# A two-layer hybrid decoder step on one core: full-height second score product, prompt values in one stage, norms first among the background stages

## The chip, the cores and the metric

The kernel runs on one core of one Trainium2 chip. The metric is the time of one execution in device microseconds (us). PE is TensorE (matmuls), DVE is VectorE, ACT is ScalarE, POOL is GpSimd and SP is SyncE, which here only issues transfers. PSUM is the memory that PE writes its results to; DVE and ACT read them from there.

## The reference, cut to what matters

One step of a two-layer decoder trunk for a prompt of 512 tokens and 32 sample tokens: layer 0 mixes tokens by gated linear attention, layer 1 by dilated windowed attention with three groups of heads, and each is followed by a gated convolutional feed-forward block. The change is in layer 1. Its scores, for each head and each group:

```python
DIL_GROUPS = ((128, 1), (512, 4), (2048, 16))          # (window, dilation)
q, k = _rmsnorm(p[:, :, :, 0], q_gain), _rmsnorm(p[:, :, :, 1], k_gain)   # per head, 64 wide
s = jnp.einsum('bhqe,bhke->bhqk', qb, kw) * DIL_SCALE + bias
p = jnp.exp(s - jnp.max(s)); den = jnp.sum(p)
o = jnp.einsum('bhqk,bhke->bqhe', p, vw) / den
out = sum over groups of softmax(log den + max) * o       # then @ w_out
```

(This is the reference's `_dil_group_prompt` and `_combine_groups` with the reshaping taken out.)

## The kernel before, in words

All activations stand transposed, 128 features on the partitions and 544 tokens (512 prompt, 32 sample) in the columns. Weights and activations are split into two float32r halves, high and low, and `product` (line 104) multiplies three of the four combinations: per block of 128 output columns of a weight and per half of the tokens it issues 24 matmuls into one PSUM buffer, tagged `ps` (three buffers). After every three of its eight steps of the contraction it calls `tick()`.

`tick()` runs the background work. There are four queues of generators, `lanes[0]` to `lanes[3]`; a tick takes them from the last to the first and lets the head of each go on to its next `yield`. Before the change `lanes[3]` holds `values`, `lanes[2]` the norms, `lanes[1]` the decode work on the key and value caches, `lanes[0]` the `attention` of one head pair and one group. The order in which instructions stand on an engine follows from the ticks and from the scheduler of the tile layer, which moves ready instructions past waiting ones; on the chip each engine takes its instructions in that order.

In `dilated` the loop over `jj` (8 head pairs of 2 heads of 64) projects q, k and v of the three groups by `product`, 9 products for each pair. For each pair there are:

- `qk_norm`, six times: the mean square over 64 features by two matmuls with a block matrix (`pn`, lines 694 and 695), a logarithm and an exponential on ACT, a multiplication on DVE.
- `attention`, three times: transposes of v (`pvt`), scores into `psc`, softmax on DVE and ACT into `ex`. For group 0 the scores are made of split operands. `split_scores` builds for each head h a q2 that holds q's high half in this head's 64 rows and q's low half in the other 64, and a k2 that holds k's high half in both, so that one matmul over 128 rows (line 798) gives high times high plus low times high. What is missing, high times low, is a second product over the 64 rows of the head (line 801), with k's low half `kl`. Both heads share one tile `kl`, each in its own 64 rows. The loop over `UNITS[0]` gives 8 matmuls of line 798 and 8 of line 801 for each pair, 2 of the 8 with 128 columns and 6 with 256.
- `values`: the three groups' softmax sums are combined (`share`), `ex` is scaled on DVE (line 873 or so), transposed by PE (`ptr`, line 892), copied from PSUM into `PT` by ACT and DVE (lines 894, 896), and multiplied with the values into one PSUM buffer `po` (line 907), 30 matmuls with 64 output rows. Group 2 uses the tile `diag`, zero outside its small blocks, in place of `PT`. The four units are (group 1), (group 2), (group 0, first half), (group 0, second half), and the line 907 matmuls of the first two stand in stage 3 of the loop over n, those of the other two in stage 5:

```python
for m in {3: (0, 1), 5: (2, 3)}.get(n, ()):
    ...
    mm(o, R[g][2][:, kb, r], PT[m][:, h, c:c + P], start=..., stop=..., skip_group_check=True)
```

So three shapes of the PE array are in use beside the full 128 rows x 128 columns of `product`: 64 rows x 128 columns (lines 796 and 801), 128 rows x 64 columns (line 907), and 128 x 32 or 64 x 32 (decode, lines 949, 959, 1004, 1009; group 2's scores, line 781). A profile row gives the shape as rows*columns.

Of the kernel before, what the change touches and what calls it, by code (L numbers as in the profile page):

```python
# [11 lines left out]
F32 = mybir.dt.float32  # L12
# [7 lines left out]
P = 128  # L20
# [16 lines left out]
def trunk(ctx: ExitStack, tc: tile.TileContext, A, O, stage=4):  # L37
# [23 lines left out]


    lanes = [deque(), deque(), deque(), deque()]
    norms = lanes[2]

    def tick():

# [570 lines left out]
    def dilated(nx, xold, tables, nxt):  # L638
        first = load_w(A["wdi"][0], KT, 256, "wdi")
        with ExitStack() as es:  # L640
# [24 lines left out]
            dma2(dmask, A["dmask"])  # L665
            diag = ac.tile([P, 2, 512], F32, name="diag")
            nc.gpsimd.memset(diag, 0.0)
            done = set()

            def upto(what):  # L670
# [54 lines left out]
            def split_scores(q, k):  # L725


                kl = at.tile([P, TP], F32R, name="kl", bufs=1)
                parts = []
                for h in range(2):  # L730
                    a, b = slice(64 * h, 64 * h + 64), slice(64 - 64 * h, 128 - 64 * h)
                    q2, k2 = [at.tile([P, TP], F32R, name=f"{n}{h}", bufs=1) for n in ("q2", "k2")]
                    nc.scalar.copy(q2[a], q[a])
                    nc.scalar.copy(k2[a], k[a])
                    nc.scalar.copy(k2[b], k[a])
                    tt(out=q2[b], in0=q[a], in1=q2[a].bitcast(F32), op=ALU.subtract)
                    tt(out=kl[a], in0=k[a], in1=k2[a].bitcast(F32), op=ALU.subtract)
                    parts.append((q2, k2, kl))
                return parts

            def softmax(st, h, todo):
# [10 lines left out]
            def attention(jj, g, q, k, v, R):  # L752

                sk, W, R_ = tables[g]
                nk = (256, P, 32)[g]
                bias = at.tile([P, 2, nk], F32, name=f"bias{g}", bufs=1)
                t = sk[:]
                dma(bias, bass.AP(t.tensor, t.offset + 2 * jj * R_ + min(nk, P) - 1, [[W, P], [R_, 2], [1, nk]]))
                vt = at.tile([P, 4, P], F32, name="vt", bufs=4)
                ps = pa.tile([P, 512], F32, name="pvt", tag="pa")  # L760
                for t in range(4):
                    nc.tensor.transpose(ps[:, t * P:(t + 1) * P], v[:, t * P:(t + 1) * P], ident)
                nc.scalar.copy(vt.rearrange("p a b -> p (a b)"), ps)
                yield
                while (jj, 1, g) not in done:
                    yield
                parts = split_scores(q, k) if g == 0 else None
                if parts:
                    yield
                    yield  # L770
                st = at.tile([P, 4, 2, 2], F32, name=f"st{g}")
                ex = []
                if g == 2:
                    ps = [pa.tile([P, 512], F32, name="psc", tag="pa") for h in range(2)]
                    ex.append(at.tile([P, 2, 4, 32], F32, name="ex2", bufs=1))
                    for t in range(4):
                        for h in range(2):
                            r = slice(64 * h, 64 * h + 64)
                            for c in range(4):
                                cc = slice(c * P + 32 * t, c * P + 32 * t + 32)  # L780
                                mm(ps[h][32 * c:32 * c + 32, 32 * t:32 * t + 32], q[r, cc], k[r, cc], start=True, stop=True)
                    for h in range(2):
                        softmax(st, h, [(t, ps[h][:, 32 * t:32 * t + 32], ex[0][:, h, t], bias[:, h]) for t in range(4)])
                        yield
                for u, todo in enumerate(UNITS[g]):
                    ps = [pa.tile([P, 512], F32, name="psc", tag="pa") for h in range(2)]
                    ex.append([at.tile([P, 512], F32, name="ex", bufs=6) for h in range(2)])

                    for part in range(2 if parts else 1):
                        for i, (t, k0, c, w) in enumerate(todo):  # L790
                            tq, tk = slice(t * P, (t + 1) * P), slice(k0 * P, k0 * P + w)
                            for h in range(2):
                                r = slice(64 * h, 64 * h + 64)
                                o = ps[h][:, c:c + w]
                                if not parts:
                                    mm(o, q[r, tq], k[r, tk], start=True, stop=True)
                                elif part == 0:
                                    mm(o, parts[h][0][:, tq], parts[h][1][:, tk], start=(i == 0), stop=False,
                                       skip_group_check=True)
                                else:  # L800
                                    mm(o, parts[h][0][r, tq], parts[h][2][r, tk], start=False, stop=True,
                                       skip_group_check=True)
                    for h in range(2):
                        softmax(st, h, [(t, ps[h][:, c:c + w], ex[u][h][:, c:c + w], bias[:, h, nk - w:])
                                        for t, k0, c, w in todo])
                        yield
                R[g] = (st, ex, vt)
                done.add(("scores", jj, g))
# [19 lines left out]
            def values(jj, R):  # L828
# [31 lines left out]
                for n in range(len(units) + 2):  # L860
# [17 lines left out]
                    if 0 <= n - 1 < len(units):  # L878
                        g, u = units[n - 1]
                        if g < 2:  # L880
                            lo = UNITS[g][u][0][2]
                            PT[n - 1] = at.tile([P, 2, 512], F32, name="PT")
                        else:
                            PT[n - 1] = diag
                            for c in range(4):
                                r = slice(32 * c, 32 * c + 32)
                                nc.vector.transpose(diag[r].rearrange("p h (t c k) -> p (h t) c k", c=4, k=32)[:, :, c],
                                                    R[g][1][0][r].rearrange("p h t k -> p (h t) k"))
                        for h in range(2 if g < 2 else 0):
                            pt = pa.tile([P, 512], F32, name="ptr", tag="pa")  # L890
                            for a in range(lo, 512, P):
                                nc.tensor.transpose(pt[:, a:a + P], R[g][1][u][h][:, a:a + P], ident)
                            if h:
                                nc.scalar.copy(PT[n - 1][:, h, lo:], pt[:, lo:])
                            else:
                                nc.vector.tensor_copy(PT[n - 1][:, h, lo:], pt[:, lo:])
                    for m in {3: (0, 1), 5: (2, 3)}.get(n, ()):
                        g, u = units[m]
                        if po is None:
                            po = pa.tile([P, 512], F32, name="po", tag="pa")  # L900
                        todo = ([(t, k0 + kk, c + kk * P) for t, k0, c, w in UNITS[g][u] for kk in range(w // P)]
                                if g < 2 else [(t, t, t * P) for t in range(4)])
                        for i, (t, kb, c) in enumerate(todo):
                            for h in range(2):
                                r = slice(64 * h, 64 * h + 64)
                                o = po[r, t * P:(t + 1) * P] if g == 0 else po[r].rearrange("p (m c r) -> p r c m", c=4, r=4)[:, t]
                                mm(o, R[g][2][:, kb, r], PT[m][:, h, c:c + P], start=(m == 0 and i == 0),
                                   stop=(m + 1 == len(units)), skip_group_check=True)
# [5 lines left out]
            def decode_scores(j, ks, pace, D):  # L914
# [1 line left out]

                bl = at.tile([P, 3, P], F32, name="bl", bufs=1)
                dma2(bl, A["dbl"][j])
                bh, bx = at.tile([P, 2, 2, P], F32R, name="b2", tag="kl", bufs=1).rearrange("p c g n -> c p g n")
                nc.scalar.copy(bh, bl[:, 1:])  # L920
                tt(out=bx, in0=bl[:, 1:], in1=bh.bitcast(F32), op=ALU.subtract)
                Sd = D["Sd"] = at.tile([P, KEYS], F32, name="Sd", bufs=1)
# [107 lines left out]
            for jj in range(KT):  # L1030
# [8 lines left out]
                for n, (c, g) in enumerate(ORDER):  # L1039
# [46 lines left out]
                    if (c, g) == (2, 2):  # L1086
                        if jj:
                            upto(("values", jj - 1))
                        lanes[3].append(values(jj, R))
                if i:  # L1090
                    lanes[1].append(decode_values(j, vs, 9 if j < 3 else 2, D))
                    upto((jj, 1, 0))
# [4 lines left out]
            ogh = [xp.tile([P, NT], F32R, name=f"xh{k}") for k in range(6)]  # L1097
            ogl = [xp.tile([P, NT], F32R, name=f"xl{k}") for k in range(6)]
            ogh += [at.tile([P, NT], F32R, name="ogh", tag="p", bufs=3) for k in range(2)]
            ogl += [at.tile([P, NT], F32R, name="ogl", tag="PT") for k in range(2)]  # L1100

            def split_og(k):
                nc.scalar.copy(ogh[k], og[k])
# [1 line left out]

            for k in range(6):
                split_og(k)
            spare = [("q20", 1), ("q21", 1), ("k20", 1), ("k21", 1), ("kl", 1)] + 3 * [("q", 3)]
            x = [None] * KT

            def old(m):
# [222 lines left out]
```

## Time and profile before

| what | value |
|---|---|
| median of 3 runs | 1783.75 us (1783.56 to 1787.02) |
| time of the profiled execution | 1782.73 us |
| its span, first to last instruction | 1781.0 us |
| granted TensorE clock, share of full speed | 0.998 |
| PE busy | 1762.5 us, 99% of the span |
| DVE busy | 1088.0 us, 61% |
| ACT busy | 802.6 us, 45% |

The span is cut by the program's stages: the first layer's mixer to about 247 us, its feed-forward block to about 672 us, the dilated layer to about 1385 us, and the last feed-forward block to the end. A matmul's row has its start and its duration from entering the array to its modelled end; matmuls overlap in the array, so the cost of one in a stream is the distance between two starts and not the duration. Plain float32 matmuls leave two records each, transposes and float32r matmuls one.

### The profile page before, as it was taken

Reading aid. Unit: us, or ns where it says so; the run is one execution under the profiler, and the core shown is the slowest. Engines: PE = TensorE matmul, PEld = TensorE weight load, DVE = VectorE, ACT = ScalarE, POOL = GpSimd, SP = SyncE. Lnnn points to the kernel's source line nnn. Section 1 sums busy time; section 2 is a strip of 40 time slices with the busy share of each in tenths; the row PEclk is TensorE's granted clock in tenths of the full one; section 3 lists DMA queues with packets and bytes.
Section 4 is the critical chain, followed back from the end, with each engine's and each line's share of the span. In section 5 each row is a group of like instructions: output and inputs, shape, how many; then the busy total and the mean of one; then the engine's idle time right before and its main releaser. Section 6 shows DMA issues by size and latency. Waiting matters only on the chain. (4 is left out here: it accounts for less than half of the span.)

```text
span 1781.0 us, 35680 instructions
## 1 busy us (share of the span) xinstructions
PE 1762.5 (99%) x14774; PEld 1672.8 (94%) x14774; DVE 1088.0 (61%) x2552; ACT 802.6 (45%) x1549; POOL 225.4 (13%) x416
## 2 busy tenths in 40 slices
PE   7999999999999999999999999999999999999999
PEld 7999999999999999988998889889888999999999
DVE  7665656764467645666575657666665666347652
ACT  5554544442244435645556465537454434224331
POOL 3000101110011110111012010211121111002100
PEclk9999999999999999999999999999999999999999
DMA  5034432432422244346436643654473222222222
GB/s 183 27 136 152 139 120 74 154 105 82 138 92 95 82 139 180 105 168 220 172 118 208 226 150 129 218 180 151 168 253 139 95 77 75 92 101 96 79 97 87
DMA packets 55266, 236.24 MB, mean 133 GB/s; under 512 B 11470, under 2 KB 20896, under 8 KB 37056
## 3 DMA queue, kind: packets, MB, share of 16 engines
q1 hardware_dynamic: 36816, 145.61, 23.6%
q0 software_dynamic: 18288, 88.36, 13.9%
q8 instruction: 116, 1.90, 0.4%
q14 instruction: 46, 0.38, 0.1%
HBM read 210.32 MB, written 29.33 MB: 135 GB/s over the span
## 5 line engine op out<-in xcount | busy, mean ns | idle before, releaser
L104 PE MATMUL ps<-xh,whi 128*128 128x256 f32 (+2 forms) x3056 | 890.1, 292 | 7.4 <-ACT xh L157 5.4
L104 PE MATMUL ps<-xl,whi 128*128 128x256 f32 (+2 forms) x3056 | 885.8, 290 | 4.0 <-DVE xl L158 4.0
L104 PE MATMUL ps<-xh,wlo 128*128 128x256 f32 (+2 forms) x3056 | 885.4, 290 | 0.7 <-DVE wlo L91 0.7
L104 PEld LDWEIGHTS ps<-xh,whi 128*128 128x128 f32 (+1 forms) x3056 | 576.6, 189 | 25.4 <-issue 15.9
L104 PEld LDWEIGHTS ps<-xl,whi 128*128 128x128 f32 (+1 forms) x3056 | 576.4, 189 | 11.7 <-DVE xl L158 5.6
L104 PEld LDWEIGHTS ps<-xh,wlo 128*128 128x128 f32 (+1 forms) x3056 | 576.2, 189 | 8.9 <-issue 5.9
L104 PE MATMUL ps<-gl,whi 128*128 128x272 f32 x704 | 198.8, 287 | 0.0
L104 PE MATMUL ps<-gh,whi 128*128 128x272 f32 x704 | 198.5, 288 | 0.3 <-DVE x L196 0.3
L104 PE MATMUL ps<-gh,wlo 128*128 128x272 f32 x704 | 195.8, 287 | 0.0
L566 DVE TENSOR_TENSOR u<-ps,rstd 128x256 f32<-128x256 f32 x176 | 74.2, 422 | 141.5 <-PE ps L104 141.1
L90 ACT CAST whi<-wu 128x1024 fp32r<-128x1024 f32 x88 | 92.4, 1050 | 98.1 <-PE ps L104 98.1
L104 PEld LDWEIGHTS ps<-gh,whi 128*128 128x128 f32 x704 | 132.2, 188 | 0.5 <-DVE x L196 0.5
L104 PEld LDWEIGHTS ps<-gl,whi 128*128 128x128 f32 x704 | 132.5, 188 | 0.0
L196 DVE TENSOR_TENSOR x<-ps,x 128x272 f32<-128x272 f32 x108 | 46.7, 439 | 140.5 <-PE ps L104 138.9
L104 PEld LDWEIGHTS ps<-gh,wlo 128*128 128x128 f32 x704 | 130.9, 188 | 0.0
L91 DVE TENSOR_TENSOR wlo<-wu,whi 128x1024 fp32r<-128x1024 f32 x88 | 107.5, 1221 | 32.7 <-ACT whi L90 32.6
L90 ACT CAST whi<-wd 128x768 fp32r<-128x768 f32 x64 | 50.1, 783 | 171.5 <-PE ps L104 142.1
L572 POOL COPY uo<-u 128x18 f32<-128x18 f32 x88 | 53.4, 607 | 401.6 <-DVE u L568 401.6
L91 DVE TENSOR_TENSOR wlo<-wdi,whi 128x1024 fp32r<-128x1024 f32 x72 | 87.9, 1221 | 18.3 <-ACT whi L90 18.2
L90 ACT CAST whi<-wdi 128x1024 fp32r<-128x1024 f32 x72 | 75.2, 1045 | 45.6 <-PE ps L104 36.8
L588 ACT CAST gh<-g 128x544 fp32r<-128x544 f32 x44 | 28.5, 647 | 132.5 <-DVE g L585 132.5
L124 ACT ACTIVATE ex<-ex,nm 128x128 f32<-128x128 f32 (+2 forms) x192 | 74.6, 390 | 25.7 <-DVE nm L748 25.7
(307 smaller groups left out, 2371.9 us busy)
## 6 DMA issues: line engine op xcount, KB each, us to landing
wu<-in_wu SPq DMA_DIRECT2D x44, 1024.0 KB, 4.8
wdi<-in_wdi SPq DMA_DIRECT2D x36, 1024.0 KB, 5.2
vc<-in_dv POOLq DMA_DIRECT2D x28, 1024.0 KB, 7.0
wd<-in_wd SPq DMA_DIRECT2D x32, 704.0 KB, 4.1
kc<-in_dkA POOLq DMA_DIRECT2D x16, 1024.0 KB, 6.5
kc<-in_dkB POOLq DMA_DIRECT2D x16, 768.0 KB, 5.2
out_vo<-v POOLq DMA_DIRECT2D x24, 256.0 KB, 3.0
out_ko<-k POOLq DMA_DIRECT2D x24, 256.0 KB, 2.7
```

The costliest lines, as they stand in the source:

```text
L90: nc.scalar.copy(hi, r)
L91: tt(out=lo, in0=r, in1=hi.bitcast(F32), op=ALU.subtract)
L104: mm(ps[:m, :b - a], ww, xx[k][:, a:b], start=(k == 0 and s == 0), stop=(k == kt - 1 and s == 2))
L124: last_exp[0] = act(out, in_, AF.Exp, **kw)
L196: tt(out=out[:, c], in0=ps, in1=old[:, c], op=ALU.add)
L566: tt(out=u[:, 2 + c0:258 + c0], in0=ps[:, :256], in1=nx.rstd[:, c0:c0 + 256], op=ALU.mult)
L572: nc.gpsimd.tensor_copy(out=uo[:, f, :].rearrange("p (b t) -> p b t", t=2), in_=u[:, 512:566].rearrange("p (b t) -> p b t", t=6)[:, :, :2])
L588: nc.scalar.copy(h_, g)
```

## The change

1. The second product of group 0's scores goes over all 128 rows. `kl` becomes two tiles `klz0` and `klz1`, one for each head, that are set to zero once at the start of `dilated` by two ACT copies from the zeroed `diag`; `split_scores` then writes only the head's own 64 rows. Line 801 (802 after) uses q2 and klz whole: the other head's 64 rows of q2 meet zeros.
2. The value products of all four units stand in stage 5. `PT` has three buffers in place of two.
3. The norms go to `lanes[3]` and `values` to `lanes[2]`, so a tick runs the norms first.
4. `b2`, which shared a buffer with `kl`, has its own. SBUF for it comes from the descriptor memory of POOL's transfers, set to 8192 bytes per partition.

```diff
     lanes = [deque(), deque(), deque(), deque()]
-    norms = lanes[2]
+    norms = lanes[3]
...
             nc.gpsimd.memset(diag, 0.0)
+            klz = [ac.tile([P, TP], F32R, name=f"klz{h}") for h in range(2)]
+            for t in klz:
+                nc.scalar.copy(t, diag[:, 0])
...
-                kl = at.tile([P, TP], F32R, name="kl", bufs=1)
...
-                    tt(out=kl[a], in0=k[a], in1=k2[a].bitcast(F32), op=ALU.subtract)
-                    parts.append((q2, k2, kl))
+                    tt(out=klz[h][a], in0=k[a], in1=k2[a].bitcast(F32), op=ALU.subtract)
+                    parts.append((q2, k2, klz[h]))
...
-                                    mm(o, parts[h][0][r, tq], parts[h][2][r, tk], start=False, stop=True,
+                                    mm(o, parts[h][0][:, tq], parts[h][2][:, tk], start=False, stop=True,
                                        skip_group_check=True)
...
-                            PT[n - 1] = at.tile([P, 2, 512], F32, name="PT")
+                            PT[n - 1] = at.tile([P, 2, 512], F32, name="PT", bufs=3)
...
-                    for m in {3: (0, 1), 5: (2, 3)}.get(n, ()):
+                    for m in {5: (0, 1, 2, 3)}.get(n, ()):
...
-                bh, bx = at.tile([P, 2, 2, P], F32R, name="b2", tag="kl", bufs=1).rearrange("p c g n -> c p g n")
+                bh, bx = at.tile([P, 2, 2, P], F32R, name="b2", bufs=1).rearrange("p c g n -> c p g n")
...
-                        lanes[3].append(values(jj, R))
+                        lanes[2].append(values(jj, R))
...
-    nc = bacc.Bacc("TRN2", target_bir_lowering=False, num_devices=1)
+    nc = bacc.Bacc("TRN2", target_bir_lowering=False, num_devices=1, dynamic_dma_scratch_size=8192)
```

The change moves instructions. On PE, in the third head pair (jj = 2) where the first half of group 0's scores stands among the products of a projection, the program has before:

```order
L104 MATMUL ps<-xl_7240,whi 128x272
L798 MATMUL psc<-k_10565,q_10564 128x128
L798 MATMUL psc<-k_10565,q_10564 128x256
L801 MATMUL psc<-kl,q_10564 128x128
L801 MATMUL psc<-kl,q_10564 128x256
L104 MATMUL ps<-xh_7239,wlo 128x272
L104 MATMUL ps<-xh_7327,whi 128x272
L104 MATMUL ps<-xl_7328,whi 128x272
L104 MATMUL ps<-xh_7327,wlo 128x272
L104 MATMUL ps<-xh_7415,whi 128x272
L798 MATMUL psc<-k_10572,q_10571 128x128
```

and now (line numbers one higher):

```order
L104 MATMUL ps<-xh_7239,wlo 128x272
L799 MATMUL psc<-k_10566,q_10565 128x128
L799 MATMUL psc<-k_10566,q_10565 128x256
L802 MATMUL psc<-klz_7650,q_10565 128x128
L802 MATMUL psc<-klz_7650,q_10565 128x256
L104 MATMUL ps<-xh_7327,whi 128x272
L104 MATMUL ps<-xl_7328,whi 128x272
L104 MATMUL ps<-xh_7327,wlo 128x272
L104 MATMUL ps<-xh_7415,whi 128x272
L104 MATMUL ps<-xl_7416,whi 128x272
L799 MATMUL psc<-k_10573,q_10572 128x128
```

The place is the same but for two products; the second score product is now of the same array shape as its neighbours (the row shows only the output's size). Over the whole program line 801's 64 matmuls stand in 25 blocks, each between matmuls of full shape; line 802's have no block of another shape.

On PE, the values of the second head pair, which run while the third is projected. Before (8 more of line 907 follow 13 rows further on, in a block of their own):

```order
L104 MATMUL ps<-xh_7239,wlo 128x256
L907 MATMUL po<-PT,vt 64x4x32
L104 MATMUL ps<-xh_7327,whi 128x256
L907 MATMUL po<-PT,vt 64x4x32 x7
L907 MATMUL po<-diag,vt 64x4x32 x8
L892 MATMUL ptr<-ident,ex 128x128 x8
L694 MATMUL pn<-sqh,blk 128x272
L695 MATMUL pn<-sql,blk 128x272
L907 MATMUL po<-PT,vt 64x128 x6
L104 MATMUL ps<-xl_7328,whi 128x256
L104 MATMUL ps<-xh_7327,wlo 128x256
```

and now:

```order
L104 MATMUL ps<-xl_7240,whi 128x256
L104 MATMUL ps<-xh_7239,wlo 128x256
L104 MATMUL ps<-xh_7327,whi 128x256
L908 MATMUL po<-PT,vt 64x4x32 x8
L908 MATMUL po<-diag,vt 64x4x32 x8
L908 MATMUL po<-PT,vt 64x128 x14
L697 MATMUL pn<-sqh,blk 128x272 x2
L104 MATMUL ps<-xl_7240,whi 128x256
L698 MATMUL pn<-sql,blk 128x272 x2
```

All 30 stand behind each other, and the transposes stand ahead of them. Over the program line 907's 240 matmuls stand in 32 blocks before, in 8 now; the blocks of the decode work with 128 x 32 go from 62 to 63.

On ACT, at the start of the dilated layer, before:

```order
L90 CAST whi<-wdi 128x1024 x2
L157 ACTIVATE xh_7591<-x,gains 128x544
L166 ACTIVATE sq<-x 128x544
L90 CAST whi<-wdi 128x1024
L181 ACTIVATE rstd<-pss,eps 128x272 x2
L124 ACTIVATE rstd<-rstd 128x544
```

and now:

```order
L90 CAST whi<-wdi 128x1024 x2
L157 ACTIVATE xh_7591<-x,gains 128x544
L166 ACTIVATE sq<-x 128x544
L670 CAST klz_7650<-diag 128x512
L670 CAST klz_7651<-diag 128x512
L90 CAST whi<-wdi 128x1024
L181 ACTIVATE rstd<-pss,eps 128x272 x2
L124 ACTIVATE rstd<-rstd 128x544
```

The two zeroing copies stand between the last square of the feed-forward block's end and the third weight split of the dilated layer.

## Rows read from the trace of the kernel before

**Rows 1.** The page: busy time of each engine (share of the span, instructions), PE's busy tenths and granted clock in 40 slices, and the chain that ended last.

```profile
PE 1762.5 (99%) x14774; PEld 1672.8 (94%) x14774; DVE 1088.0 (61%) x2552; ACT 802.6 (45%) x1549; POOL 225.4 (13%) x416
...
PEclk9999999999999999999999999999999999999999
...
PE 23%; ACT 0%; issue 0%; DVE 0%; DVEq 0%
```

**Rows 2.** Busy time of PE and granted clock in stretches: the dilated layer without its ends, and its end.

```profile
675.00:1350.00 675.00, 673.27 (x6165) 1.00 0.50 177
...
1355.00:1390.00 35.00, 32.15 (x250) 1.00 0.21 77
```

**Rows 3.** Who PE waited for between 675 and 1350 us: us in total, times, longest.

```profile
PE pdo L1009 <- DMA vc<-in_dv: 1.0, 2, 0.8
PE ptr L892 <- DVE ex L873: 0.4, 1, 0.4
PE po L907 <- DVE PT L896: 0.3, 1, 0.3
```

**Rows 4.** Timeline of PE, three products in a stream with 256 columns, and the first of the next with 288 columns (start us, duration us).

```profile
856.59 0.28 PE L104 MATMUL ps<-xh,whi 128*128 128x256 f32 x1
...
857.53 0.28 PE L104 MATMUL ps<-xh,wlo 128*128 128x256 f32 x1
857.64 0.29 PE L104 MATMUL ps<-xh,whi 128*128 128x288 f32 x1
```

**Rows 5.** Timeline of PE around the first half of group 0's scores, third head pair.

```profile
904.52 0.29 PE L104 MATMUL ps<-xh,whi 128*128 128x272 f32 x1
904.65 0.29 PE L104 MATMUL ps<-xl,whi 128*128 128x272 f32 x1
904.78 0.39 PE L798 MATMUL psc<-k,q 128*128 128x128 f32 x2
905.10 0.49 PE L801 MATMUL psc<-kl,q 64*128 64x128 f32 x2
905.52 0.40 PE L104 MATMUL ps<-xh,wlo 128*128 128x272 f32 x1
905.75 0.29 PE L104 MATMUL ps<-xh,whi 128*128 128x272 f32 x1
```

**Rows 6.** Timeline of PE, the second half of group 0's scores of the same pair, 256 columns each.

```profile
910.08 0.71 PE L798 MATMUL psc<-k,q 128*128 128x256 f32 x4
910.73 0.50 PE L801 MATMUL psc<-kl,q 64*128 64x256 f32 x4
911.16 0.39 PE L694 MATMUL pn<-sqh,blk 128*128 128x272 f32 x1
```

**Rows 7.** Timeline of PE through the values of the second head pair, line 907's records two for each matmul.

```profile
851.60 0.43 PE L907 MATMUL po<-PT,vt 128*64 128x128 f32 x2
851.96 0.38 PE L104 MATMUL ps<-xh,whi 128*128 128x256 f32 x1
852.27 0.98 PE L907 MATMUL po<-PT,vt 128*64 128x128 f32 x13
...
855.22 0.29 PE L695 MATMUL pn<-sql,blk 128*128 128x272 f32 x1
855.44 0.88 PE L907 MATMUL po<-PT,vt 128*64 128x128 f32 x12
856.25 0.39 PE L104 MATMUL ps<-xl,whi 128*128 128x256 f32 x1
...
857.90 0.29 PE L695 MATMUL pn<-sql,blk 128*128 128x272 f32 x1
858.11 1.09 PE L907 MATMUL po<-PT,vt 128*64 128x128 f32 x16
859.14 0.40 PE L104 MATMUL ps<-xl,whi 128*128 128x288 f32 x1
```

**Rows 8.** The copies of `PT` from PSUM: count, ns of one (min/median/max), first and last start us, forms.

```profile
L894 ACT COPY PT<-ptr x24: 458/586/591, 770.5 to 1348.5; 128x512 f32<-128x512 f32 x16, 128x384 f32<-128x384 f32 x8
L896 DVE COPY PT<-ptr x24: 542/683/692, 773.6 to 1348.1; 128x512 f32<-128x512 f32 x16, 128x384 f32<-128x384 f32 x8
```

**Rows 9.** Timeline of ACT and of POOL at the start of the dilated layer (in brackets the idle time before and what ended it).

```profile
673.13 0.64 ACT L166 ACTIVATE sq<-x 128x544 f32<-128x544 f32 x1
677.81 1.05 ACT L90 CAST whi<-wdi 128x1024 fp32r<-128x1024 f32 x1 [4.04 <-issue]
...
668.37 0.99 POOL L667 MEMSET diag<- 128x1024 f32 x1
```

**Rows 10.** DVE's part in the norms, and whom DVE waited for between 675 and 1350 us.

```profile
L705 DVE SCALAR_TENSOR_TENSOR k<-p,qkg,sq x24: 740/1125/1151, 719.7 to 1304.0; 128x512 f32<-128x512 f32 x24
...
DVE p L189 <- PE ps L104: 51.8, 42, 3.7
```

More of the change, by code (lines that the diff above doesn't have):

```diff
@@ L1099, in dilated @@
             ogh += [at.tile([P, NT], F32R, name="ogh", tag="p", bufs=3) for k in range(2)]
-            ogl += [at.tile([P, NT], F32R, name="ogl", tag="PT") for k in range(2)]
+            ogl += [at.tile([P, NT], F32R, name="ogl", tag="PT", bufs=3) for k in range(2)]
             def split_og(k):
@@ L1107, in dilated @@
                 split_og(k)
-            spare = [("q20", 1), ("q21", 1), ("k20", 1), ("k21", 1), ("kl", 1)] + 3 * [("q", 3)]
+            spare = [("q20", 1), ("q21", 1), ("k20", 1), ("k21", 1), ("b2", 1)] + 3 * [("q", 3)]
             x = [None] * KT
```

## Prediction

> **What bounds the kernel now.** I read the page first. PE is busy 99% of the span, DVE 61%, ACT 45%, and the chain that ended last is PE's with line 104 in nearly all of it; the granted clock is the upper of its two levels, 2.4 GHz, in every slice [rows 1]. So the question is what the change does to PE's own time. I then cut out the dilated layer, the only place where the program's order differs: between 675 and 1350 us PE is busy 673.27 of 675 us [rows 2], and it waited there for other engines and transfers 1.7 us in all [rows 3]. Nothing is to be won by making another engine faster. But "busy" also holds time in which the array does not take in columns, so I went to the timeline and read distances between starts.
>
> In a stream of 256-column products there are 9 starts from 856.59 to 857.64, 1.05 us, which is 0.117 us each [rows 4]; with 272 columns it is 0.125 to 0.13, as the first rows of the next view show [rows 5]. A matmul of full shape costs that and no more, whichever weights it loads. Where the shape of the array changes, the distances grow, and that is what the prediction rests on.
>
> **The second score product, before.** In the first half of a unit's scores two of line 798 and two of line 801 (128 and 256 columns each) take from 904.78 to 905.52, 0.74 us [rows 5]. In full shape the same four would be two of 256 columns at 0.117 and two of 128, which I put at 0.06, half of that (an estimate) [rows 4]: 0.36 us. One thing may stay. Line 801 waits for DVE's low half, and a matmul that waits can't have its weights loaded ahead. What that costs I take from the second half: four of line 798, with the step into the other shape at their end, take 910.08 to 910.73, 0.65 us, against 4 x 0.117 = 0.47 [rows 6]. The 0.18 left are the step in shape and one late weight load, 0.09 each if shared evenly (the step alone is 0.09 to 0.10 in the values, below). So after the change the first half costs 0.36 to 0.45 and saves 0.29 to 0.38 us. There are two for each head pair, one per head.
>
> In the second half eight matmuls take from 910.08 to 911.16, 1.08 us [rows 6]. After: 8 x 0.117 = 0.94, or 1.03 with the late load. It saves 0.05 to 0.14 us only. The four of line 801 take 0.43 us with the step back included, so about 0.34 without it, where four of full height take 0.47: here the two heads' halves of the array work beside each other, and the change gives that up.
>
> For each pair: 2 x (0.29 to 0.38) + 0.05 to 0.14 = 0.63 to 0.90 us. The wait for DVE does not go away, so I stay below the middle, 0.72. Times 8 pairs: **5.8 us** saved (5.0 to 7.2).
>
> Against this stands a rule. The Trainium skill, page "TensorE: Matmul & The Clock Gate", Part 3 (packing small matmuls), says that a matmul with few rows takes as long as one of full height, and that what is won is that matmuls on different row groups run beside each other, with starts up to 4 ns apart. By that rule alone the padding only loses. It would cost 0.117 us for each pair of heads that overlaps, 16 pairs in the 8 second halves, 1.9 us; the trace shows the overlap in the second halves, and in the first halves two matmuls of one head behind each other, where nothing overlaps.
>
> **The values in one stage.** A block of line 907 of 16 records takes 858.11 to 859.14, 1.03 us; one of 12 records 855.44 to 856.25, 0.81 us [rows 7]. Four records more are 0.22 us, so a record costs 0.055 us and the block has 1.03 - 16 x 0.055 = 0.15 us on top, at its end. At its start the matmul ahead of it takes 0.22 and 0.21 us (855.22 to 855.44, 857.90 to 858.11) in place of 0.125: 0.09 us. A block thus costs 0.24 us beside its work. Before there are 32 blocks, four for each pair, now 8. 24 x 0.245 = **5.9 us** saved. Bounds: 0.20 us (4.8 us) if part of a block's end is a wait that stays; 0.30 us (7.2 us), since the block of two records at 851.60 costs more (0.36 us to the next start, against 0.11 for its records, and 0.31 for the product behind it in place of 0.117) [rows 7].
>
> What could wait in the merged block is the copy of the last `PT`. Of the 30 matmuls 22 are of earlier units: 44 records x 0.055 = 2.4 us stand between the block's start and the first that reads the last `PT`, and some products stand between the last transposes and the block. Two copies of 0.59 (ACT) and 0.68 us (DVE) go beside each other [rows 8]. That is hidden. Without that cover, at most the DVE copy, 0.7 us for each pair, 5.5 us in all.
>
> **Norms first.** The matmuls of the norms are of full shape, their number is the same, and they move by a few products. What changes is who is first on DVE and ACT in a tick. I cost it at nothing: DVE waits 51.8 us for PE's products in this layer before it can take them out of PSUM [rows 10], so it is ahead of PE. Cover gone, a k norm of 1.13 us [rows 10] ahead of such a read would delay it, but a PSUM buffer is needed again only two products of 24 matmuls later, 2 x 24 x 0.125 = 6 us. In the new order decode has one block more, at the price of one of line 907's: **0.25 us** lost.
>
> **The rest.** The two zeroing copies: ACT is idle for 4.04 us exactly where they stand, from 673.77 to 677.81, and `diag` is zero from 669.36 on [rows 9]. Two casts of 512 columns take at most 2 x 0.64 us, by the row of the square of 544 columns: nothing, and 1.3 us once if `diag` were late. `b2` with its own buffer takes away a wait that ACT, not PE, had; nothing. The smaller descriptor memory has no row in this trace; POOL is 13% busy [rows 1], and PE's whole wait for a POOL transfer is 1.0 us [rows 3]: nothing, up to a doubling of that 1.0 us. The end of the layer (35 us with 32.15 busy) [rows 2] has the same number of products between the last values and the last weights; nothing.
>
> **Sum.** -5.8 - 5.9 + 0.25 = -11.4 us. The profiled execution took 1782.73 us around its span of 1781.0, so 1771.3 us, with a span of about 1769.6. The median of the runs lies 1.0 us above the profiled execution: **1772.3 us**. With the bounds, -9.5 to -14.2: 1769.6 to 1774.2 for this case alone.
>
> **Rivals.** (A) The above.
>
> (B) As a mechanism of this kernel: the long distances at line 801 are the wait for the split and its late weight load, not the shape, and they stay, while the overlap in the second halves goes. Then the score part costs 1.9 us in place of saving 5.8: -5.9 + 1.9 + 0.25 = -3.7, 1780.0 us. The page of the Trainium skill named above stands on this side. For it: line 801 does wait for DVE. Against: the distance behind line 801, where nothing waits, is long too (905.52 to 905.75 and the 0.42 us that two matmuls of 128 and 256 columns take) [rows 5].
>
> (C) Norms first makes DVE or ACT late for something that PE needs soon. The four waits of [rows 3] are 0.43 us each on average; one such wait at a quarter of the 48 norms is 12 x 0.4 = 4.8 us: 1777.1 us. Against: the idle time of DVE in [rows 10].
>
> (D) The other side: the merged block. PE takes instructions in order, so a late scaling, transpose or `PT` copy of any unit now holds back all 30 matmuls and the projection behind them. The gain is eaten at 11.4 / 8 = 1.43 us for each pair, and the kernel is slower by over 0.2% from 1.9 us. A fully exposed chain of one scale, one copy on DVE (0.68) and one on ACT (0.59), about 2.0 us with the transposes between, gives +16 us: 1788.3 us. For it: [rows 3] has one wait of 0.4 us and one of 0.3 us of just this kind. Against: they are once in 8 pairs, and the new order has the transposes further ahead.
>
> (E) It does not do what it says: the blocks merge, but the shorter PE time is waited out elsewhere, at the weights' transfers or at the end of the layer. No wait for a projection's weights stands in [rows 3], and 11 us in 675 are 1.6% more demand. 1783.0 us.
>
> **Chances.** A 0.79, B 0.07, C 0.07, D 0.03, E 0.04. The likeliest is 1772.3 us. The range takes in A with its bounds, C, and B: 1768.5 to 1780 us. Less than 0.2%, 3.6 us, can't be told from no change here. Faster by more: A, C and half of B, 0.89; within: the other half of B and E, 0.07 (B lies on the border); slower 0.04.
>
> **What would show it.** Right: no row of 64*128 at line 802, and the four of a first half within 0.36 to 0.45 us; one block of 60 records of line 908 for each pair, about 60 x 0.055 + 0.15 = 3.45 us; PE busy in the dilated layer shorter by about 11 us, with its waits still under 3 us, and the other three stages unchanged. Wrong: PE rows waiting for `PT`, `ex` or `klz`, a first half of scores that still takes 0.7 us, or a dilated layer that is shorter while another stage is longer.

## The result, and the profile after

The changed kernel takes 1765.43 us (median of 5 runs, 1764.82 to 1767.99) against 1783.75 us: a ratio of 0.9897 with a 95% interval of 0.9884 to 0.9911, or 18.3 us less. The direction was right and the size was not: 11.4 us were forecast, and the time lies 3 us under the range of 1768.5 to 1780 us. The profiled execution took 1765.01 us, its span 1763.2 us, 17.8 less than before.

The page after, with the lines that answer to [rows 1]; the columns are the same.

```profile
span 1763.2 us, 35656 instructions
...
PE 1744.2 (99%) x14774; PEld 1668.1 (95%) x14774; DVE 1085.1 (62%) x2552; ACT 803.4 (46%) x1551; POOL 224.7 (13%) x416
...
PEclk9999999999999999999999999999999999999999
```

PE has the same 14774 matmul records and is 18.3 us less busy; its clock is the same, and ACT has the two zeroing copies more. PE's busy time between 675 and 1350 us, and whom it waited for there, against [rows 2, 3]:

```profile
675.00:1350.00 675.00, 672.13 (x6287) 1.00 0.51 179
...
PE pdo L1010 <- DMA vc<-in_dv: 2.0, 1, 2.0
PE ps L104 <- DVE x L196: 0.8, 1, 0.8
```

The waits are 2.8 us in place of 1.7, so no stall went away; 122 more records fit into the same stretch (6287 against 6165). The time is gone from between the matmuls. The three places of the prediction, on PE's timeline after (start us, duration us). A first half of group 0's scores, against [rows 5]:

```profile
899.29 0.29 PE L104 MATMUL ps<-xh,wlo 128*128 128x272 f32 x1
899.42 0.39 PE L799 MATMUL psc<-k,q 128*128 128x128 f32 x2
899.65 0.39 PE L802 MATMUL psc<-klz,q 128*128 128x128 f32 x2
899.88 0.29 PE L104 MATMUL ps<-xh,whi 128*128 128x272 f32 x1
900.00 0.29 PE L104 MATMUL ps<-xl,whi 128*128 128x272 f32 x1
```

From the first matmul of the scores to the product behind them 0.46 us in place of 0.74. And from that product to the next one 0.12 us, where [rows 5] has 0.23 (905.52 to 905.75). A second half, against [rows 6]:

```profile
903.83 0.72 PE L799 MATMUL psc<-k,q 128*128 128x256 f32 x4
904.38 0.63 PE L802 MATMUL psc<-klz,q 128*128 128x256 f32 x4
904.86 0.29 PE L697 MATMUL pn<-sqh,blk 128*128 128x272 f32 x1
904.98 0.29 PE L698 MATMUL pn<-sql,blk 128*128 128x272 f32 x1
```

1.03 us in place of 1.08, and again 0.12 us to the matmul after, not the 0.23 that stood there before. [rows 6] ends at 911.16; the next row of before is

```profile
911.39 0.29 PE L695 MATMUL pn<-sql,blk 128*128 128x272 f32 x1
```

Where the 0.23 comes from can be seen on PEld, the weight loads. Before, around [rows 5], and after, around the first half above:

```profile
905.10 0.29 PEld L801 LDWEIGHTS psc<-kl,q 64*128 64x128 f32 x2
905.52 0.19 PEld L104 LDWEIGHTS ps<-xh,wlo 128*128 128x128 f32 x1
905.62 0.19 PEld L104 LDWEIGHTS ps<-xh,whi 128*128 128x128 f32 x1
...
899.53 0.31 PEld L802 LDWEIGHTS psc<-klz,q 128*128 128x128 f32 x2
899.76 0.19 PEld L104 LDWEIGHTS ps<-xh,whi 128*128 128x128 f32 x1
899.88 0.19 PEld L104 LDWEIGHTS ps<-xl,whi 128*128 128x128 f32 x1
```

After, the weights of the product at 899.88 are loaded from 899.76 on, 0.12 us ahead. Before, the load of the product at 905.52 starts with it, the next load 0.10 us later, and so the next product starts only at 905.75. In the layer of before this is so at every return to full shape from 32 or 64 rows or columns: 120 of 120 loads start within 0.02 us of their matmul, while in full shape behind full shape, float32 transposes among them, 4 of 4228 do. After, there are 74 such returns.

The values of the second pair, against [rows 7]:

```profile
849.37 0.28 PE L104 MATMUL ps<-xh,whi 128*128 128x256 f32 x1
849.58 1.09 PE L908 MATMUL po<-PT,vt 128*64 128x128 f32 x16
850.50 1.04 PE L908 MATMUL po<-diag,vt 128*64 128x128 f32 x16
...
851.37 1.70 PE L908 MATMUL po<-PT,vt 128*64 128x128 f32 x28
853.00 0.52 PE L697 MATMUL pn<-sqh,blk 128*128 128x272 f32 x2
853.36 0.28 PE L104 MATMUL ps<-xl,whi 128*128 128x256 f32 x1
```

One block of 60 records in 3.42 us, and behind it two matmuls in 0.36 us where two in a stream take 0.25.

To add this up over the layer, the distance from each matmul to the next start goes to a group. A product of full shape keeps its plain distance (0.118, 0.125 or 0.132 us by its columns); what it takes longer just ahead of a block of another kind, or within the two starts behind one, goes to that block's group. "Rest" is transposes, late loads of the norms, the other two groups' scores and decode's small products in full shape. Two things that differ from execution to execution stand by themselves: "waits" is PE's idle time of over 0.1 us, the end of the layer included, and "1.2 GHz" is what a fall of the granted clock cost. All of it is counted from the traces between the same two products of the dilated layer, us:

| kernel | scores of group 0 | values | decode | rest | waits | 1.2 GHz | layer |
|---|---|---|---|---|---|---|---|
| before | 23.6 | 37.3 | 75.1 | 59.1 | 3.0 | 0 | 691.8 |
| after | 15.9 | 28.8 | 75.6 | 58.2 | 2.9 | 0 | 674.9 |
| e1_score | 15.5 | 35.6 | 69.6 | 59.4 | 2.6 | 0 | 676.4 |
| e2_values | 23.5 | 30.4 | 75.0 | 59.8 | 3.7 | 1.7 | 687.8 |
| e3_norms | 23.7 | 38.0 | 71.0 | 59.4 | 5.8 | 1.7 | 693.3 |
| e4_nowait | 22.7 | 35.4 | 72.6 | 59.6 | 3.6 | 1.7 | 689.3 |
| e5_four | 15.7 | 40.7 | 71.1 | 60.8 | 2.8 | 1.7 | 686.5 |
| e6_full | 15.9 | 53.7 | 73.0 | 57.9 | 2.2 | 1.7 | 698.0 |
| e7_quads | 16.0 | 28.8 | 68.2 | 58.1 | 3.2 | 0 | 667.9 |
| e9_before_quads | 23.9 | 37.2 | 67.0 | 59.0 | 6.0 | 1.7 | 688.5 |
| e10_pairs | 15.9 | 28.8 | 66.8 | 58.6 | 2.9 | 0 | 666.7 |
| e11_quads_score | 15.8 | 39.1 | 68.0 | 58.5 | 2.6 | 0 | 677.7 |
| e12_quads_values | 23.8 | 30.4 | 68.1 | 60.2 | 4.7 | 0 | 680.8 |

(493.6 us of plain products are in each layer.) Before to after: scores -7.7, values -8.5, everything else -0.6. Of the span's 17.8 us, 0.9 lie in the stages ahead, where the two programs are the same: so much do two executions differ anyway. Each row is one execution, and times below are medians of several, which can differ from it by 2 to 4 us.

In six of the traces the granted clock falls from its upper level to the lower one, 1.2 GHz, for 3.4 us near the end of the layer. In e2_values:

```profile
1338.00:1341.54 3.54, 1.21 (x11) 1.00 1.01 394
1341.54:1344.95 3.41, 3.41 (x27) 0.50 0.09 37
```

Matmuls take twice as long there (a transpose 0.21 us to the next start in place of 0.11), so half of the 3.4 us is counted as lost. In each of the six PE had just waited for a transfer of decode's, for 2.0 to 3.8 us; waits of 2.0 us in the kernel after and 2.4 us in e7_quads were not followed by a fall.

### The profile page after: what moved, and what is told of

Same layout as the page of the kernel before. It is cut to its first block, busy times and chain, and to the rows that moved or that the text cites. A ratio compares the mean times of both kernels' runs of the same rounds, so it can differ in the third digit from the quotient of the medians.

```text
span 1763.2 us, 35656 instructions
## 1 busy us (share of the span) xinstructions
PE 1744.2 (99%) x14774; PEld 1668.1 (95%) x14774; DVE 1085.1 (62%) x2552; ACT 803.4 (46%) x1551; POOL 224.7 (13%) x416
## 3 DMA queue, kind: packets, MB, share of 16 engines
q0 software_dynamic: 18288, 88.36, 14.2%
## 4 chain that ended last, share of the span: by engine, by line
PE 93%; issue 4%; DMA 2%; POOL 1%; ACT 0%; DVE 0%; SPq 0%; DVEq 0%; POOLq 0%
PE ps L104 80%; PE pd L950 2%; PE pdo L1010 2%; PE po L908 2%; PE ptr L893 1%; PE pn L697 1%; PE pn L698 1%; PE pvt L764 1%; DMA vc<-in_dv 1%; PE psc L797 0%; DMA wv<-in_wg 0%; PE psc L799 0%; PE psc L802 0%; PE psc L783 0%; DMA out_sgs<-S 0%
```

## The experiments

The first four run the parts of the change alone, or leave out a wait. Theory S: each block of another array shape also delays the second matmul behind it; that is the step from 0.125 to 0.23 us seen above, 0.105 us. Theory N: the missing microseconds come from the norms going first. Theory W: the wait for the split, not the shape, makes line 801 slow. How much faster a kernel is goes by the ratio of the runs, times the median of the kernel before in the same comparison.

**e1_score**, the second score product alone:

```diff
-                                    mm(o, parts[h][0][r, tq], parts[h][2][r, tk], start=False, stop=True,
+                                    mm(o, parts[h][0][:, tq], parts[h][2][:, tk], start=False, stop=True,
...
-                    parts.append((q2, k2, kl))
+                    parts.append((q2, k2, klz[h]))
```

> The kernel before with only the second score product changed (full height against zeros, own buffer for b2, smaller descriptor memory); values in two stages, lanes as before. Blocks of another array shape that go straight back to full shape fall from 132 to 101 in the program's order: 25 of the scores, 6 of other work that the scheduler regroups. Theory S (each block of another shape also delays the matmul after the next, by a late weight load of 0.105 us, so that a block costs about 0.35 us and not 0.245): 5.8 + 25 x 0.105 = 8.4 us from the scores and 6 x 0.35 = 2.1 from the rest, 10.5 us faster than before, about 1773.3. Theory N (blocks cost what the prediction said, and the rest of the gain comes from the norms going first): 5.8 + 6 x 0.245 = 7.3 us, about 1776.5. Theory W (the long distances at the score product are the wait for its split): 1.9 us slower from the scores, about 1784.

Measured 1767.52 us against 1784.5, ratio 0.9913 (0.9898 to 0.9927), 15.5 us faster: more than any theory said. The table splits it: the scores give 8.1 us (S: 8.4; N: 5.8), the values 1.7 with three blocks fewer, and decode 5.5, which nobody had forecast. W is out. The decode part is taken up in e7 and e9.

**e2_values**, the values in one stage alone:

```diff
-                            PT[n - 1] = at.tile([P, 2, 512], F32, name="PT")
+                            PT[n - 1] = at.tile([P, 2, 512], F32, name="PT", bufs=3)
...
-                    for m in {3: (0, 1), 5: (2, 3)}.get(n, ()):
+                    for m in {5: (0, 1, 2, 3)}.get(n, ()):
```

> The kernel before with only the values' products of all four units in one stage (three PT buffers, smaller descriptor memory). Blocks of 128 x 64 fall from 36 to 15 and exits to full shape from 132 to 115. Theory S: 17 to 21 blocks x 0.35 = 6.0 to 7.4 us faster, about 1777. Theory N: 17 to 21 x 0.245 = 4.2 to 5.1 us, about 1779.

Measured 1778.80 us, ratio 0.9965 (0.9953 to 0.9978), 6.2 us faster, as S has it. The values' own gain in the trace is 6.9 us for 21 blocks, 0.33 each, and the rest loses 0.7.

**e3_norms**, the lanes alone:

```diff
-    norms = lanes[2]
+    norms = lanes[3]
...
-                        lanes[3].append(values(jj, R))
+                        lanes[2].append(values(jj, R))
```

> The kernel before with only the lanes of norms and values exchanged. Exits to full shape fall from 132 to 128. Theory S: 4 x 0.35 = 1.4 us faster, about 1782.4. Theory N: the missing 5 to 7 us are here, about 1777 to 1779.

Measured 1781.88 us, ratio 0.9989 (0.9979 to 0.9998), 2.0 us (0.4 to 3.8) faster. Its one trace has a layer 1.5 us longer, but with 2.8 us more of waits and 1.7 of the lower clock; the work is 3.1 us shorter, most of it in decode (see e7 and e9). N falls. For the values the lanes are worth something only beside e2: with the values merged and the lanes as before there are 11 blocks of values and 30.4 us, with both 8 blocks and 28.8 us.

**e4_nowait**, the low half of k a constant zero tile, so that the second product waits for no split. It leaves out the product of q's high with k's low half and DVE's 16 splits of it:

```diff
+            klc = ac.tile([P, TP], F32R, name="klc")
+            nc.scalar.copy(klc, diag[:, 0])
...
-                    tt(out=kl[a], in0=k[a], in1=k2[a].bitcast(F32), op=ALU.subtract)
-                    parts.append((q2, k2, kl))
+                    parts.append((q2, k2, klc))
```

> The kernel before, but the low half of k for group 0 is a tile of zeros written once at the start and never again: the second score product keeps its 64-row shape and its number, and waits for no split (the scores lack the product of q's high with k's low half; DVE has 16 instructions of 0.69 us less). Exits to full shape 128 against 132. Theory S: the shape costs, not the wait: 16 late weight loads of 0.09 us at most and 4 blocks, 1.4 to 2.8 us faster, 1781 to 1782.4. Theory W: the wait costs: the whole gain of the score part, 6 us or more, comes without any change of shape, about 1777 or below.

Measured 1778.54 us, ratio 0.9966 (0.9954 to 0.9977), 6.0 us faster, more than S allowed. But it is not where W wants it: the scores give 0.9 us. A first half without the wait takes as long as in [rows 5], 0.74 us and then 0.23:

```profile
901.28 0.39 PE L798 MATMUL psc<-k,q 128*128 128x128 f32 x2
901.60 0.49 PE L801 MATMUL psc<-klc,q 64*128 64x128 f32 x2
902.03 0.40 PE L104 MATMUL ps<-xh,wlo 128*128 128x272 f32 x1
902.26 0.29 PE L104 MATMUL ps<-xh,whi 128*128 128x272 f32 x1
```

So 64 rows still cost 22.7 us without the wait, and the same products in full height 15.5 (e1). The rest of the 6.0 us comes with the new order that the scheduler made. In the trace the values are 1.9 us shorter (29 blocks in place of 32), decode 2.5 (two tears of the kind shown under e9 in place of six), and the stages ahead 1.1; a fall of the clock hides 1.7 of it. What `b2` in a buffer that the scores no longer use has to do with that order is not shown.

**e5_four**, the changed kernel with the values in four stages:

```diff
-                    for m in {5: (0, 1, 2, 3)}.get(n, ()):
+                    for m in {2: (0,), 3: (1,), 4: (2,), 5: (3,)}.get(n, ()):
```

> The changed kernel, but the values' products in four stages, one for each unit (nothing else differs). Blocks of 128 x 64 go from 12 to 49 and exits to full shape from 85 to 121; of decode's groups of four with 512 columns, one is torn apart by other work in place of seven. Theory S (a block costs 0.35 us): 36 x 0.35 = 12.6 us lost, 7 - 1 = 6 torn groups x 0.45 = 2.7 won: 9.9 us slower than the changed kernel, 8.4 us faster than before. With 0.245 us for a block: 8.8 - 2.7 = 6.1 us slower than the changed kernel, 12.2 us faster than before. If blocks cost nothing and the gain is from elsewhere: no slower than the changed kernel.

Measured 1776.22 us, ratio 0.9947 (0.9934 to 0.9959): 9.5 us faster than before, where the changed kernel was 18.3. Putting the blocks back gives back 8.9 us (S: 9.9, the prediction's price: 6.1). In the trace the values rise by 11.9 us for 37 blocks, 0.32 us each, and decode falls by 4.5, with one torn group in place of seven.

**e9_before_quads** and **e7_quads** follow the surprise of e1. Decode multiplies in groups of four matmuls, each using 32 columns of the array. In the kernel before, one such group of 512 columns stands torn in three, with two records for each of its matmuls:

```profile
893.26 1.05 PE L1009 MATMUL pdo<-vc,PTd 128*32 128x512 f32 x4
894.25 0.52 PE L694 MATMUL pn<-sqh,blk 128*128 128x272 f32 x2
894.70 1.05 PE L1009 MATMUL pdo<-vc,PTd 128*32 128x512 f32 x2
895.67 0.40 PE L104 MATMUL ps<-xh,wlo 128*128 128x272 f32 x1
...
900.44 1.05 PE L1009 MATMUL pdo<-vc,PTd 128*32 128x512 f32 x2
901.41 0.39 PE L104 MATMUL ps<-xh,whi 128*128 128x272 f32 x1
```

The first two matmuls take 0.99 us to the next start, the third 0.97, and the fourth, 5 us later, 0.97. In e7 a whole group takes 1.00:

```profile
889.09 1.07 PE L1016 MATMUL pdo<-vc,PTd 128*32 128x512 f32 x8
890.09 0.52 PE L697 MATMUL pn<-sqh,blk 128*128 128x272 f32 x2
```

So a quarter or a half costs as much as the whole. Such groups of 512 columns are torn 6 times before (three groups, twice each), 7 times after, and not once in e1; the narrower groups are torn 8 times in each of the kernels before and after. Both experiments tie the group:

```diff
+            def quad(issue):
+                first = issue(0)
+                with tc.issue_after(first.ins), tc.high_priority(offset=3000):
+                    for qd in range(1, 4):
+                        issue(qd)
```

> The kernel before with decode's groups of four tied together, and nothing else. Torn groups of 512 columns 6 to 0, exits to full shape 132 to 125. Theory Q: 6 x 0.447 + 7 x 0.35 = 5.1 us faster than before. If the tearing costs nothing but its blocks: 2.5 us; without either: as before.

Measured 1776.43 us against 1785.85, ratio 0.9953 (0.9940 to 0.9965), 8.4 us faster; in the trace decode gives 8.1. Theory Q is right in direction and, with 5.1 us, too small. (The trace's layer is only 3.3 us shorter: it has 3.0 us more of waits, and the lower clock.)

> The changed kernel, with decode's groups of four matmuls (one for each 32 columns of the array) tied together, so that the scheduler puts nothing between them. Theory Q (a torn group of 512 columns loses the overlap, one more 0.447 us, as single distances of 976 ns in place of 529 show): 7 x 0.447 + 2 blocks x 0.35 = 3.8 us faster than the changed kernel, 22 us faster than before, about 1762. If tearing costs nothing: as the changed kernel, 18 us faster than before.

Measured 1758.42 us, ratio 0.9850 (0.9836 to 0.9863), 26.8 us faster than before and 8.4 more than the change alone. Decode falls by 7.4 us, about 1 us for each of the seven tears, as the rows above say; I had allowed 0.45 for each, and 0.7 for two blocks. The tears of the narrower groups are in the 7.4 us too; what they cost was not taken apart. This kernel is faster than the change and than the kernel before.

**e6_full** was to carry the idea on: the values' products in full shape too, with each head's values padded to 128 columns.

```diff
-                                mm(o, R[g][2][:, kb, r], PT[m][:, h, c:c + P], start=(m == 0 and i == 0),
+                                mm(o, R[g][2][:, kb, h], PT[m][:, h, c:c + P], start=(m == 0 and i == 0 and h == 0),
```

> The changed kernel, but the values' products in full shape too: each head's values stand in 128 columns of which the other head's 64 are zeros (four fixed tiles, zeroed once; 24 more ACT copies of half the size), in two stages as before the change and with two PT buffers; descriptor memory 4096 bytes. Exits to full shape 76 against 85. Theory S: 9 x 0.35 = 3.1 us faster than the changed kernel, and one torn group less, 0.4: about 1762, 22 us faster than before. Theory T (the 64-column form is worth something in itself, as its weight load is shorter, 137 against 188 ns): no faster than the changed kernel.

Measured 1788.23 us, ratio 1.0016 (1.0006 to 1.0025): 2.8 us slower than before, 21 slower than the change. Theory T has the sign right, for another reason than it gave:

```profile
855.10 1.95 PE L914 MATMUL po<-PT,vtz 128*128 128x128 f32 x16
856.88 1.95 PE L914 MATMUL po<-diag,vtz 128*128 128x128 f32 x16
858.59 0.37 PE L701 MATMUL pn<-sqh,blk 128*128 128x272 f32 x1
```

32 records, 16 matmuls, take 3.49 us, 0.218 us for a matmul. In the changed kernel 60 records take 3.42, 0.114 for a matmul. The two heads' halves of the array had overlapped all along: their records start in pairs, under 0.01 us apart. I had read their 0.055 us for a record as a plain rate. 240 x 0.104 = 25 us lost, and the values' column of the table rises by 24.9.

**e11_quads_score** and **e12_quads_values** repeat e1 and e2 with the groups tied (the diffs are those above), so that no group torn by chance stands in the comparison. The tied kernel before, e9, ran in another comparison, so a difference to it is less sure than one to the kernel before.

> The kernel before with decode's groups of four tied together and with the second score product in full height, the values in two stages and the lanes as before: what the score product is worth when no group of decode is torn by chance. Against the tied kernel before (8.4 us faster than before): scores 23.6 to 15.7 us by the traces so far, 8 us won; the scheduler makes 7 blocks more of other work, 7 x 0.35 = 2.5 lost: 5.5 us faster than it, about 14 us faster than before. If the 16 us of the score product alone were all its own: 24 us faster than before.

Measured 1769.22 us against 1783.81, ratio 0.9924 (0.9910 to 0.9938), 13.6 us faster than before, 5.2 faster than the tied kernel before, where 5.5 were expected. In the trace the scores give 8.1 us, while the values, now in 35 blocks, lose 1.9 and decode 1.0.

> The kernel before with decode's groups of four tied together and with the values' products in one stage. Against the tied kernel before: 21 blocks of 128 x 64 less at 0.37 us, 7.8 us won; 6 blocks of decode more at 0.35, 2.1 lost: 5.7 us faster than it, about 14 us faster than before. By the 0.245 us of the prediction: 3.7 us faster than it, 12 us faster than before.

Measured 1772.10 us, ratio 0.9934 (0.9921 to 0.9947), 11.8 us faster, 3.4 faster than the tied kernel before: by time nearer to the prediction's price, by trace 6.8 us for 21 blocks of values, 0.32 each, with 2.3 of it lost to decode and the rest. The two parts, 5.2 and 3.4, do not add up to the 18.4 us between e9 and e7. The largest piece of what is missing is in the values: 35 blocks in e11, 11 in e12, 8 in e7. The remainder stays open.

**e10_pairs** ties the groups of one stage to each other as well:

```diff
+            def quad(issue, first=None):
+                qd0 = 0
+                if first is None:
+                    first, qd0 = issue(0), 1
...
+                    fst = None if t % 2 == 0 else fst
```

> The changed kernel with decode's groups of four tied together, and the two groups (or more) of one stage tied to each other as well. Exits to full shape 79 against 83 for the kernel with the groups alone tied. By blocks: 4 x 0.35 = 1.4 us faster than that, 28 us faster than before. Rival: PE now stands before a transfer that has not landed, since the scheduler had parted the groups for that; then waits of PE for the caches' tiles appear and it is slower than the kernel with the groups alone tied (27 us faster than before).

Measured 1759.17 us, ratio 0.9860 (0.9846 to 0.9874), 24.9 us faster than before. The intervals of e7 and e10 overlap; nothing can be told between them, nor between the two expectations.

## Why the prediction was wrong in its size

- **PE's own time decides, other engines don't**: right. No wait was removed: between 675 and 1350 us 2.8 us of waits stand where 1.7 stood.
- **The scores after**: the numbers are right by luck. Forecast were 0.36 to 0.45 us for a first half and 0.94 to 1.03 for a second, the upper ends with a late weight load behind the wait for the split; measured 0.46 and 1.03. But the wait costs nothing: without it (e4) a first half takes the same 0.74 us as before. What the estimate had wrong is the matmul of 128 columns, put at 0.06 us. Two of line 799 by themselves, which do not read k's low half, with 128 and 256 columns, take 0.23 us in the kernel after, not 0.18:

```profile
1295.44 0.40 PE L799 MATMUL psc<-k,q 128*128 128x128 f32 x2
1295.67 0.29 PE L104 MATMUL ps<-xh,whi 128*128 128x272 f32 x1
```

  A first half has two such pairs: 0.46. In a second half the extra 0.08 us lie in the first four matmuls, behind the transposes (903.83 to 904.38, 0.55), and not in the four of the split (0.48). So a head pair saves 2 x 0.28 + 0.05 = 0.61 us there, 4.9 us in all and not 5.8.
- **The scores before, the failed term**: the prediction stopped counting at the first product behind the block. The second one comes late too: 905.52 to 905.75 is 0.23 us and not 0.125 [rows 5]. It even quoted that distance, against rival B, and left it out of the sum. 25 blocks x 0.105 = 2.6 us; 4.9 + 2.6 = 7.5 against 7.7 to 8.1 measured.
- **The values' block after**: right, 3.42 us for 3.45 forecast.
- **The price of a values block, the same failed term**: 0.245 us forecast. Measured 8.5 us / 24 = 0.35 before to after, and 0.32 to 0.33 in e2, e5 and e12. In [rows 7] the product behind a block starts at 856.25, and the next one 0.22 us later in place of 0.117:

```profile
856.47 0.28 PE L104 MATMUL ps<-xh,wlo 128*128 128x256 f32 x1
```

  24 x 0.105 = 2.5 us; 5.9 + 2.5 = 8.4 against 8.5 measured.
- **Together**: the step that failed is the count of what a block costs, which stopped one matmul too early: 0.245 us where the runs show 0.32 to 0.35. With it, and with the scores as measured, 7.5 + 8.4 = 15.9 us; the layer lost 16.9 in the traces, 0.9 of it in the column "rest". The remaining 0.9 us of the span lie ahead of the layer, in equal programs.
- **Bounds**: 9.5 to 14.2 us were to hold this case. All of them were made from the entry and the end of a block, so they could not see the distance behind.
- **Norms first, cost nothing**: nearly so alone (2.0 us faster, 0.4 to 3.8). That it keeps the merged block in one piece (8 blocks in place of e2's 11) was not seen.
- **Decode's one block more, 0.25 us lost**: 75.1 to 75.6 us. That decode holds seven tears, 7.4 us to be had, was not seen.
- **Zeroing copies, nothing**: right. They stand in ACT's idle stretch, and 3.00 us of it are left:

```profile
672.83 1.13 ACT L670 CAST klz<-diag 128x512 fp32r<-128x512 f32 x2
676.96 1.05 ACT L90 CAST whi<-wdi 128x1024 fp32r<-128x1024 f32 x1 [3.00 <-issue]
```

- **The rivals**: B's mechanism is refuted: the long distances are gone in e1, and in e4 they stay without the wait. Its rule, from the Trainium skill, page "TensorE: Matmul & The Clock Gate", is no rule for the first halves, where no two matmuls of different heads stand beside each other, and its 1.9 us for the second halves is in the sum. (That a small matmul alone takes as long as a full one stands in that page's closing table, under "Why this matters for your kernels", and not in Part 3.) But e6 shows the same page of the Trainium skill right where it counts: halves that overlap are worth 25 us here. The trace agrees with it there, 0.114 against 0.218 us for a matmul, and so do decode's groups, where one matmul alone took 0.97 us and four 1.00. The overlapping pairs of line 801 start 3 to 4 ns apart in the trace, those of line 907 7 ns. C and D did not happen: PE has no wait for `PT`, `ex` or the split after. Nor did E: 16.9 of the span's 17.8 us are gone in the layer itself.

## What to carry to other kernels

Where PE is busy all the time, look at the distances between starts around each change of array shape, and count until the distance is plain again: on entry, at the end, and at the second matmul behind. Padding a small matmul to full shape paid here where its partner did not run beside it anyway (scores, 23.6 to 15.9 us), and cost nearly double where it did (values, 28.8 to 53.7 us); the timeline shows which. See in the scheduled order that matmuls which overlap stand next to each other, and tie them if the scheduler tears them. Before two traces are compared, take out the waits and the stretches at the lower clock: here they moved a layer by up to 4.7 us.

## What the runs showed of the hardware that I had not expected

- A block of another array shape costs 0.32 to 0.35 us here for the values: 0.09 at the entry, 0.15 within it and at its end, 0.105 at the second matmul behind it.
- In a stream of one shape a weight load starts about 0.12 us ahead of its matmul. At a return to full shape it started with its matmul, in 120 of 120 cases before, and the second matmul behind came 0.105 us late.
- A part of a group of overlapping matmuls costs as much as the whole: with 128 x 32 and 512 columns one matmul alone took 0.97 us, two 0.99, four 1.00.
- A plain float32 matmul of 128 columns in full shape takes 0.218 us, nearly four times what I estimated for a float32r one (0.06) and about twice what such a one took (0.23 for the pair above, of which 0.117 are the 256 columns).
- Near the end of the layer the granted clock fell to 1.2 GHz for 3.4 us in six of thirteen traces, each time after PE had waited 2.0 to 3.8 us, though not after every such wait; it cost 1.7 us.
